# A change of order in the attention loop of a hybrid decoder layer: the last unit's scaling ahead of its neighbours, low parts and weight splits behind the probabilities

## The chip, the cores and the metric

The kernel runs on one core of a Trainium2 chip. TensorE (PE; its weight loads are listed apart as PEld), VectorE (DVE), ScalarE (ACT), GpSimd (POOL) and SyncE (SP, which here issues DMAs) each work through an instruction queue of their own and wait for one another through semaphores. The metric is the device time of one execution in microseconds; lower is better.

## The reference

One layer of a decoder for 2048 prompt tokens and 8 × 8 sample tokens. An input projection feeds a sliding-window attention (window 128, 8 query heads, 2 key heads, a learned sink per head) and a gated linear attention; both go through an output projection and are followed by a squared-ReLU MLP. The change touches the first part:

```python
h = rms_norm(x, g_mix_pre)
proj = jnp.einsum('btd,de->bte', h, w_in)
q, k, v, gq, gk, gv, gr, glr = jnp.split(proj, points, axis=-1)
q, k = rope(q...), rope(k...)
...
scores = jnp.where(mask, q @ k.T * HEAD_DIM ** -0.5, -jnp.inf)   # per head, blocks of 128
m = jnp.maximum(jnp.max(scores, axis=-1, keepdims=True), sink)
p = jnp.exp(scores - m)
p = p / (jnp.sum(p, axis=-1, keepdims=True) + jnp.exp(sink - m))
out = p @ v
```

All of it is float32. The kernel multiplies on TensorE with operands that are split into a high part and a low part (the remainder), and adds the products of the parts.

## The kernel before

The 2048 prompt tokens are 16 tiles of 128. The loop `for i in range(NB)` makes one pass per tile; what is called pass i below is the stretch from the transposes of the keys of tile i to those of tile i + 1, so it holds the last two units of tile i − 1 and the first two of tile i, and a start of the third.

**Units.** The attention of a tile is four units u0 to u3, each of two heads: `unit(i, r, jj)`, with names such as `s_7_0_0` for u0 of tile 7. A unit is a generator, and each `next` writes one step: the sink into a column of `s` (POOL); the scores `sc` (four matmuls); the row maxima `m` (two custom VectorE operations, which also write `s`); the exponentials (two on ScalarE, `s<-s,m`, each with its sum into `den`); the reciprocal of `den` and the scaling of `s` (VectorE; in u0 and u3 one of the two heads on ScalarE); the transposes `pT`; their high part `ph` (ScalarE); their low part `pl` (VectorE); the products with the values, `av` (four matmuls); half of `av` copied to `rest` (ScalarE); the sum `mo` (VectorE). Three units are under way at a time, named `behind`, `now` and `ahead` in the loop.

**Between the units.** For TensorE, `run(fill, n)` writes the next n products of the input projection of a tile further on (24 for each of its two column chunks, `proj_9_0` and `proj_9_1` for tile 9). `A_FILL` gives three numbers for each unit. A chunk's PSUM bank has tag "a", of which there are two, so the first product of a chunk needs the bank of the chunk before the last to have been read. The first unit's 11 products end with the first of a new chunk.

For the other engines, `A_PLAN` places named pieces of work at a phase (T, A, X, S, B or C, in this order) of a unit; `do(u, phase)` writes what is due:

- `first` and `rest` copy a projected tile out of PSUM, scaled by its norm `rstd_all` (ScalarE; `rest` is qk 128x248, glr and vv). `vl` writes the low parts of the values and of the gate's ranks (VectorE, vv and glr); these read the same bank.
- `turn` is the rotary step (`rotate`, GpSimd). Then `heads_T` transposes the turned queries (`pq`) and keys (`pk`) on TensorE; `lo0` and `lo1` write the queries' low parts from `pq` (VectorE, `qh<-pq,qh` and `ql<-pq,ql`), `klo0` and `klo1` the keys'.
- `x_half` transposes half of an input tile (`xT`), ScalarE takes the high part `xh`, and `x0` and `x1` are the low parts `xl` (VectorE). `xT` and `pq` have tag "d", which has a single PSUM bank.
- `junk` and `rstd` make the norm: ScalarE squares, VectorE writes `rs_v`, GpSimd writes `rstd_all`.

`split_some(n)` splits n chunks of a later projection's weights (`wg`): the early ones, 16 in all, by a GpSimd multiplication with the norm's gain, a high part on ScalarE and a low part on GpSimd; the late ones by ScalarE and VectorE.

**What sets the order.** TensorE, VectorE and ScalarE run what is written through `te`, `dv` and `ac` in the order in which it is written. GpSimd, SyncE and what is written directly to `nc.vector` (such as `load_consts`, a preparation of constants) are placed by a scheduler.

Of the kernel before, what the change touches and what calls it, by code (L numbers as in the profile page):

```python
# [25 lines left out]
NB = T // P  # L26
# [8 lines left out]
NTILE = NB + 1  # L35
# [18 lines left out]
H_EARLY, H_LATE = (1, 2), (5, 7, 6, 4, 3)  # L54
G_EARLY, G_LATE = (0, 1), (2, 3)
A_FILL = ((11, 2, 0), (10, 0, 2), (10, 0, 0), (12, 1, 0))
A_LEAD, A_SPLIT = 14, (2, 1, 0, 0)
A_PLAN = [(name, (int(at[0]), at[1])) for name, at in dict(
    klo0="3T", first="1B", hi1="3C", x1="1B", lo1="0A", klo1="0B", x0="0C", rest="3A", lo0="3A", junk="2A", turn="1A", rstd="1A", vl="3S"
).items()]  # L60
G_FIRST = (0, 1)
G_NEXT = (NB, *range(2, NB))
# [53 lines left out]
def f32(ap):  # L116
    return ap.bitcast(F32)
# [23 lines left out]
def hybrid_step_kernel(ctx: ExitStack, tc: tile.TileContext, I, O):  # L141
    nc = tc.nc
    xp = I["x_prompt"].flatten_outer_dims()
    xs = I["x_sample"].flatten_outer_dims()
    w_in = I["w_in"][0]
# [8 lines left out]
    def rows(i):  # L154
        return min(P, NTOK - i * P)

    def x_rows(i):
        return xp[i * P : (i + 1) * P, :] if i < NB else xs
# [62 lines left out]
    def split_gained(wh, wl, raw, k):  # L221
# [2 lines left out]
        ac.activation(wh, raw, AF.Copy, scale=g)  # L224
        dv.scalar_tensor_tensor(wl, raw, g, f32(wh), op0=ALU.mult, op1=ALU.subtract)

    def load_raw(stg, k, c0, n, name, tag="w_raw", bufs=2):
        raw = stg.tile([P, n], F32, tag=tag, name=f"{name}_raw{k}", bufs=bufs)
        r = slice(k * P, (k + 1) * P)
        m = min(n, G_AT - c0) if c0 < G_AT else n  # L230
        nc.sync.dma_start(raw[:, :m], w_in[r, c0 : c0 + m])
        if m < n:
            nc.sync.dma_start(raw[:, m:], w_in[r, G_AT + G_W :])
        return raw
# [13 lines left out]
    def open_gw(chunks):  # L248
        p_ = open_pool(f"g_w{chunks[0]}", "right")
        for c in chunks:  # L250
            gw[c] = (p_, *(p_.tile([P, KT, G_N], F32R, tag=f"w{c}{u}", name=f"wg{c}_{u}") for u in range(2)))
        return p_

    def load_gw(c, k, *stage):
        return c, k, load_raw(sp, k, G_AT + c * G_N, G_N, f"wg{c}", *stage)

    def split_gw(c, k, raw):
        if c in G_LATE:
            split_gained(gw[c][1][:, k, :], gw[c][2][:, k, :], raw, k)
            return  # L260
        nc.gpsimd.tensor_tensor(raw, raw, gcol[:, k : k + 1].to_broadcast([P, G_N]), op=ALU.mult)
        ac.activation(gw[c][1][:, k, :], raw, AF.Copy)
        nc.gpsimd.tensor_tensor(gw[c][2][:, k, :], raw, f32(gw[c][1][:, k, :]), op=ALU.subtract)
# [19 lines left out]
    def load_x(i):  # L283
        xs_in[i] = x = sp.tile([P, D], F32, tag="x", name=f"x_{i}", bufs=2)
        nc.sync.dma_start(x[: rows(i)], x_rows(i))
        ropes[i] = sp.tile([P, 2, HD], F32, tag="rope", name=f"rope_{i}", bufs=4)
        nc.sync.dma_start(ropes[i], I["c_rope"][i])
# [32 lines left out]
    def store():  # L320

        for dst, src in stores:
            nc.sync.dma_start(dst, src)
        stores.clear()
# [349 lines left out]
    def run(products, n=None):  # L674
        deque(products if n is None else islice(products, n), 0)
# [87 lines left out]
    def split_some(n):  # L763

        for _ in range(min(n, len(weights))):
            c, k, raw, stage = weights.popleft()
            split_gw(c, k, raw)
            if stage and late:
                weights.append((*load_gw(*late.popleft(), *stage), stage))

    early, late = (deque((c, k) for c in cs for k in range(KT)) for cs in (G_EARLY, G_LATE))
    weights = deque()
    fill = chain.from_iterable(project(i, c) for i in range(2, NTILE) for c in range(2))
# [16 lines left out]
    now, ahead, behind = next(queue), next(queue), iter(())  # L790
# [1 line left out]
        next(unit_)  # L792
    todo = {}
    for i in range(NB):
        if i + 4 < NTILE:
            load_x(i + 4)
        if i == NB - 1:
            wa_pool.release()
            w_pools.append(open_gw(G_LATE))
            for n in range(4):  # L800
                stage = ("w_raw", 2) if n % 2 else ("x", 2)
                weights.append((*load_gw(*late.popleft(), *stage), stage))
        elif i >= 3:
            for _ in range(min(2, len(early))):
                weights.append((*load_gw(*early.popleft()), None))
        store()
        if i == 4:
            nc.sync.dma_start(gain_d.rearrange("a d -> (a d)"), I["g_mix_post"][0])
            wgk, msk, smsk, dmsk, onehot, ggla = load_consts()
        if i == NB - 4:  # L810
            nc.sync.dma_start(smask, I["c_smask"])
            cached.update({(name, 0): load_cache(name, 0) for name in "kv"})
        if i >= NB - 2:
            t = i - NB + 2
            gxTs[t] = load_T(t, x_place(t))
            fill = chain(fill, projecting(t, gxTs[t], G_EARLY, ac))
        new = i + 3 < NTILE
        todo["turn"] = lambda: run(rotate(i + 1))
        if i + 2 < NTILE:
            todo["first"] = lambda: take_first(i + 2)  # L820
            todo["rest"] = lambda: todo.update(vl=take_rest(i + 2))
        if new:
            todo["junk"] = lambda: todo.update(rstd=x_norm(i + 3))

        def do(u, phase):
            for name, at in A_PLAN:
                if at == (u, phase) and name in todo:
                    todo.pop(name)()

        for u in range(4):  # L830
            next(now)
            do(u, "T")
            next(behind, None)
            next(now)
            do(u, "A")
            later = next(queue)
            next(later)
            run(fill, A_FILL[u][0])
            next(behind, None)
            if u != 3:  # L840
                next(behind, None)
            run(fill, A_FILL[u][1])
            if u == 0:
                next(now)
            if u < 2 and new:
                hi, todo[f"x{u}"] = x_half(i + 3, u)
                hi()
            elif u == 2:
                todo.update(heads_T(i + 1))
            do(u, "X")  # L850
            run(fill, A_FILL[u][2])
            if u:
                next(now)
            do(u, "S")
            if u == 3:
                next(behind, None)
            next(behind, None)
            next(ahead)
            next(now)
            do(u, "B")  # L860
            split_some(A_SPLIT[u] if i < NB - 1 else 1)
            next(now)
            do(u, "C")
            behind, now, ahead = now, ahead, later
# [3 lines left out]
    fill = chain(fill, *(projecting(t, gxTs[t], G_LATE, ac) for t in G_FIRST))  # L868
# [21 lines left out]
    for n in range(4):  # L890
# [23 lines left out]
        behind, now, ahead = now, ahead, later  # L914
# [489 lines left out]
    early = []  # L1404
    fill = chain(ending_, products())
# [451 lines left out]
    turn = [0]  # L1857
# [304 lines left out]
```

## Time and profile before

| | us |
|---|---|
| median of three runs | 2213.25 (2213.18 to 2215.95) |
| the profiled execution | 2212.31 |
| its span, from first to last instruction | 2210.4 |
| one pass of the attention loop (pass 7, 150.66 to 167.07) | 16.41 |
| passes 1 to 15, from the keys' transposes of tile 1 to those of the sample tile behind tile 15 | 48.27 to 296.60 |

The profiled execution is 0.9 us below the median of the runs. In it the granted TensorE clock is 0.995. A row of a timeline gives the start (us from the span's start), the duration, engine, line, operation, output<-inputs and the tile's shape; several alike in a row have a count, and in brackets stands the idle time ahead and what ended it. Buffer numbers are left out of the names. Nearly all rows have line 130, that of the helper that keeps the order. VectorE and ScalarE overlap the end of one instruction with the start of the next, so what one instruction costs its successor is the distance of the starts.

### The profile page before, as it was taken

What the parts mean: (1) busy time and instruction counts of PE and PEld (TensorE: products, weight loads), DVE (VectorE), ACT (ScalarE), POOL (GpSimd) and SP (SyncE); (2) the same over time, 40 slices, a digit from 0 to 9 for tenths busy, and PEclk for the clock granted to TensorE, in tenths of its full rate; (3) what the DMA queues carried; (4) which work ended last, traced back from release to release, by engine and by line L of the source; (5) the groups of instructions that cost most, each with busy time, mean ns of one, the idle gap of its engine ahead of it and who ended that gap; (6) DMA issues with size and microseconds to landing.
All of it is one profiled execution on the core that took longest, in us unless ns stands there. A gap on an engine that the chain in (4) does not pass through costs nothing.

```text
span 2210.4 us, 34115 instructions
## 1 busy us (share of the span) xinstructions
PE 2166.2 (98%) x11784; PEld 1864.2 (84%) x11784; DVE 1530.4 (69%) x3101; ACT 1220.3 (55%) x2626; POOL 262.3 (12%) x418
## 2 busy tenths in 40 slices
PE   8999999999999999899999999999999999999998
PEld 7989989999997788688888887888888888888886
DVE  5888868777785665788888655547776666555566
ACT  5889867566664443555555544435455444454454
POOL 3576512111111010000000000000000000000000
PEclk9999999999999999999999999999999999999999
DMA  7344332224336665768777677768553344666685
GB/s 228 131 143 149 102 104 65 68 80 142 126 125 219 214 217 181 240 226 274 256 271 255 248 228 225 246 187 264 175 204 139 137 154 148 229 203 197 191 271 186
DMA packets 240185, 411.53 MB, mean 186 GB/s; under 512 B 25924, under 2 KB 142124, under 8 KB 235900
## 3 DMA queue, kind: packets, MB, share of 16 engines
q1 hardware_dynamic: 240012, 409.35, 55.8%
q8 instruction: 93, 1.52, 0.3%
q14 instruction: 80, 0.66, 0.1%
HBM read 266.34 MB, written 143.99 MB: 186 GB/s over the span
## 4 chain that ended last, share of the span: by engine, by line
PE 83%; DVE 7%; ACT 5%; DMA 2%; issue 2%; POOL 1%; SPq 0%; DVEq 0%; ACTq 0%; POOLq 0%
PE dn L130 27%; PE gproj L130 9%; PE uc L130 7%; PE ua L130 7%; PE out L1306 6%; PE proj L130 5%; PE ud L130 4%; PE ub L130 4%; PE ue L130 4%; PE sam L130 1%; PE dsam L130 1%; PE av L130 1%; PE o L130 1%; PE pT L130 1%; PE sc L130 1%
## 5 line engine op out<-in xcount | busy, mean ns | idle before, releaser
L130 PE MATMUL dn<-o0t,o0s 128*128 128x512 f32 x896 | 349.1, 390 | 1.7 <-ACT f L1936 1.5
L130 PE MATMUL dn<-o1t,o0s 128*128 128x512 f32 x896 | 349.5, 390 | 0.3 <-DVE o1t L219 0.2
L130 PE MATMUL dn<-o0t,o1s 128*128 128x512 f32 x896 | 349.3, 390 | 0.0
L219 DVE TENSOR_TENSOR o1s<-rs,o0s 128x512 fp32r<-128x512 f32 x224 | 154.6, 691 | 231.0 <-ACT o0s L218 224.8
L218 ACT ACTIVATE o0s<-rs 128x512 fp32r<-128x512 f32 x224 | 141.1, 631 | 306.2 <-PE dn L130 284.0
L130 PE MATMUL gproj<-wg,gxh 128*128 128x384 f32 x1024 | 272.4, 342 | 0.3 <-DVE gp_s L213 0.3
L130 ACT ACTIVATE st<-st 128x512 f32<-128x512 f32 x224 | 141.2, 630 | 141.8 <-DVE st L130 137.8
L130 PEld LDWEIGHTS dn<-o0t,o0s 128*128 128x128 f32 x896 | 168.2, 188 | 38.6 <-ACT f L1936 1.9
L130 PEld LDWEIGHTS dn<-o1t,o0s 128*128 128x128 f32 x896 | 168.2, 188 | 37.1 <-DVE o1t L219 1.1
L130 PEld LDWEIGHTS dn<-o0t,o1s 128*128 128x128 f32 x896 | 168.2, 188 | 35.4
L130 PE MATMUL uc<-H,s 128*128 128x512 f32 x768 | 188.5, 394 | 1.7 <-ACT s L130 1.2
L130 PEld LDWEIGHTS gproj<-wg,gxh 128*128 128x128 f32 x1024 | 183.8, 188 | 4.1 <-issue 3.1
L130 PE MATMUL gproj<-wg,gxl 128*128 128x384 f32 x576 | 186.0, 340 | 0.2 <-DVE gp_s L213 0.2
L130 PE MATMUL ua<-H,w 128*128 128x512 f32 x744 | 179.2, 390 | 0.0
L130 PEld LDWEIGHTS uc<-H,s 128*128 128x128 f32 x768 | 144.2, 189 | 33.2 <-ACT s L130 1.6
L130 PEld LDWEIGHTS ua<-H,w 128*128 128x128 f32 x744 | 139.7, 188 | 29.4
L1306 PE MATMUL out<-wo,mt 128*128 128x512 f32 x680 | 160.4, 394 | 2.6 <-ACT mt L218 1.5
L219 DVE TENSOR_TENSOR o1t<-rt,o0t 128x512 fp32r<-128x512 f32 x224 | 153.3, 684 | 6.7 <-ACT o0t L218 6.7
L208 POOL TENSOR_TENSOR frs<-rs_v,half 128x1 f32<-128x1 f32 (+1 forms) x13 | 10.1, 787 | 1213.5 <-DVE rs_v L206 693.1
L1306 PEld LDWEIGHTS out<-wo,mt 128*128 128x128 f32 x680 | 127.4, 189 | 29.6 <-ACT mt L218 1.9
L218 ACT ACTIVATE o0t<-rt 128x512 fp32r<-128x512 f32 x224 | 138.3, 618 | 6.7 <-PE dn L130 3.1
L130 DVE TENSOR_TENSOR st<-st 128x512 f32<-128x512 f32 x160 | 110.6, 691 | 26.9 <-ACT st L130 22.6
(398 smaller groups left out, 4318.0 us busy)
## 6 DMA issues: line engine op xcount, KB each, us to landing
s_d<-st SPq DMA_DIRECT2D x32, 1792.0 KB, 8.5
rs<-s_d SPq DMA_DIRECT2D x224, 256.0 KB, 3.0
raw<-in_w_up SPq DMA_DIRECT2D x64, 512.0 KB, 4.4
rt<-t_d SPq DMA_DIRECT2D x128, 256.0 KB, 3.9
rt<-in_w_down SPq DMA_DIRECT2D x96, 256.0 KB, 2.8
t<-in_w_down SPq DMA_DIRECT2D x64, 256.0 KB, 3.9
t_d<-t SPq DMA_DIRECT2D x32, 512.0 KB, 3.2
hraw<-h_d SPq DMA_DIRECT2D x20, 512.0 KB, 5.4
```

The lines of the kernel that those rows point to most:

```text
L130: ins = call(*a, **k)
L208: nc.gpsimd.tensor_tensor(out, v[:n], e, op=ALU.pow)
L218: nc.scalar.activation(hi, src, AF.Copy)
L219: vector.tensor_tensor(lo, src, f32(hi), op=ALU.subtract)
L1306: te.matmul(banks[c], x, w[:, c * 512 : (c + 1) * 512], start=k + u == 0, stop=k == KT - 1 and u == len(products) - 1,)
```

## The change

Six entries and a few lines move. `rest` and `lo0` go from phase A of u3 to its phase S, behind the scaling; `vl` from phase S of u3 to phase A of the next tile's u0; `lo1` from phase A of u0 to phase S; `x0` from phase C of u0 to phase A of u1. In u3 the scores of the next unit are written behind the transposes of the unit in place of ahead of them. The weight splits move from behind phase B to behind phase A of a unit, and in all passes but the last two of them from u0 to u1. The last pass has a fill table of its own. An early pair of weight chunks is loaded ahead of the input tile.

```diff
-A_LEAD, A_SPLIT = 14, (2, 1, 0, 0)
+A_LAST = ((9, 0, 4), *A_FILL[1:])
+A_LEAD, A_SPLIT = 14, (0, 2, 1, 0)
...
-    klo0="3T", first="1B", hi1="3C", x1="1B", lo1="0A", klo1="0B", x0="0C", rest="3A", lo0="3A", junk="2A", turn="1A", rstd="1A", vl="3S"
+    klo0="3T", first="1B", hi1="3C", x1="1B", lo1="0S", klo1="0B", x0="1A", rest="3S", lo0="3S", junk="2A", turn="1A", rstd="1A", vl="0A"
...
+    fetched = []
...
-        nc.sync.dma_start(raw[:, :m], w_in[r, c0 : c0 + m])
+        fetched[:] = [nc.sync.dma_start(raw[:, :m], w_in[r, c0 : c0 + m])]
...
     for i in range(NB):
-        if i + 4 < NTILE:
+        if 3 <= i < NB - 1 and early:
+            for _ in range(min(2, len(early))):
+                weights.append((*load_gw(*early.popleft()), None))
+            with tc.issue_after(fetched[0].ins):
+                load_x(i + 4)
+        elif i + 4 < NTILE:
             load_x(i + 4)
...
-        elif i >= 3:
-            for _ in range(min(2, len(early))):
-                weights.append((*load_gw(*early.popleft()), None))
...
+        fills = A_FILL if i < NB - 1 else A_LAST
         for u in range(4):
             next(now)
             do(u, "T")
             next(behind, None)
             next(now)
             do(u, "A")
+            split_some(A_SPLIT[u] if i < NB - 1 else 1)
             later = next(queue)
             next(later)
-            run(fill, A_FILL[u][0])
+            run(fill, fills[u][0])
...
             do(u, "S")
             if u == 3:
                 next(behind, None)
             next(behind, None)
-            next(ahead)
+            if u != 3:
+                next(ahead)
             next(now)
+            if u == 3:
+                next(ahead)
             do(u, "B")
-            split_some(A_SPLIT[u] if i < NB - 1 else 1)
             next(now)
             do(u, "C")
```

In the following lists of instructions the number behind a name's unit or tile is a buffer's; `ISA` is the custom operation of the row maxima.

VectorE, from the low part of the probabilities of u3 of tile 6 to the row maxima of u1 of tile 7, before:

```order
L130 TENSOR_TENSOR pl_6_1_1_2355<-pT_6_1_1_2349,ph_6_1_1_2354 128x512
L130 SCALAR_TENSOR_TENSOR ql_7_2275<-pq_7_2267,ql_7_2275 64x512
L130 RECIPROCAL den_7_0_0_2373<-den_7_0_0_2373 128x2
L130 TENSOR_SCALAR s_7_0_0_2247<-s_7_0_0_2247,den_7_0_0_2373 128x256
L130 TENSOR_TENSOR mo_6_1984<-av_6_1_1_2391,rest_6_1_1_2396 64x256
L130 TENSOR_TENSOR kl_7_2277<-pk_7_2272,kh_7_2276 64x128
L130 TENSOR_TENSOR xl_10_2404<-xT_10_0_2405,xh_10_2403 128x512
L130 ISA s_7_0_1_2316,m_7_0_1_2434<-sc_7_0_1_2412,amask_215,sink_418 128x256
```

and after:

```order
L131 TENSOR_TENSOR pl_6_1_1_2353<-pT_6_1_1_2342,ph_6_1_1_2352 128x512
L131 SCALAR_TENSOR_TENSOR vv_8_2336<-proj_8_1_2126,rstd_all_184,vv_8_2336 128x2x64
L131 SCALAR_TENSOR_TENSOR glr_202<-proj_8_1_2126,rstd_all_184,glr_202 128x16
L131 RECIPROCAL den_7_0_0_2371<-den_7_0_0_2371 128x2
L131 TENSOR_SCALAR s_7_0_0_2247<-s_7_0_0_2247,den_7_0_0_2371 128x256
L131 SCALAR_TENSOR_TENSOR ql_7_2275<-pq_7_2267,ql_7_2275 64x512
L131 TENSOR_TENSOR mo_6_1984<-av_6_1_1_2390,rest_6_1_1_2395 64x256
L131 TENSOR_TENSOR kl_7_2277<-pk_7_2272,kh_7_2276 64x128
L131 ISA s_7_0_1_2311,m_7_0_1_2427<-sc_7_0_1_2412,amask_215,sink_418 128x256
```

The lows of tile 8's values and ranks have come in, the reading of `pq_7` by `ql_7` stands three rows further back, and the input's low part has left.

TensorE around the first transposes of an input, u0 of tile 7, has this order in both kernels (here of after):

```order
L131 MATMUL proj_9_0_2258<-wa_hi_197,xl_9_2141 128x392
L131 MATMUL proj_9_1_2388<-wa_hi_197,xh_9_2140 128x392
L131 MATMUL av_6_1_1_2390<-ph_6_1_1_2352,vv_5_1517 128x256
L131 MATMUL av_6_1_1_2390<-pl_6_1_1_2353,vv_5_1517 64x256
L131 MATMUL av_6_1_1_2390<-pl_6_1_1_2353,vv_6_1812 64x256
L131 MATMUL av_6_1_1_2390<-ph_6_1_1_2352,vv_6_1812 128x256
L131 MATMUL proj_9_1_2388<-wa_lo_198,xh_9_2140 128x392
L131 MATMUL proj_9_1_2388<-wa_hi_197,xl_9_2141 128x392
L131 MATMUL xT_10_0_2404<-ident_177,x_10_2098 128x128 x4
L131 MATMUL sc_7_0_1_2412<-kh_7_2276,qh_7_2274 128x256
```

Nothing moves here; the second row is the eleventh product of u0, which takes the bank of `proj_8_1`, and `xT_10_0` takes the bank of `pq_7`.

ScalarE, from the exponentials of u3 of tile 6 to the high part of its transposes, before:

```order
L130 ACTIVATE s_6_1_1_2189,den_6_1_1_2308<-s_6_1_1_2189,m_6_1_1_2302 128x257 x2
L130 ACTIVATE qk_8_2230<-proj_8_1_2127,rstd_all_184 128x248
L130 ACTIVATE glr_202<-proj_8_1_2127,rstd_all_184 128x2x16
L130 ACTIVATE vv_8_2313<-proj_8_1_2127,rstd_all_184 128x2x64
L130 ACTIVATE s_6_1_1_2189<-s_6_1_1_2189,den_6_1_1_2308 128x256
L130 ACTIVATE rest_6_1_0_2341<-av_6_1_0_2330 64x256
L130 ACTIVATE ph_6_1_1_2354<-pT_6_1_1_2349 128x512
```

and after:

```order
L131 ACTIVATE s_6_1_1_2189,den_6_1_1_2308<-s_6_1_1_2189,m_6_1_1_2302 128x257 x2
L131 ACTIVATE s_6_1_1_2189<-s_6_1_1_2189,den_6_1_1_2308 128x256
L131 ACTIVATE qk_8_2230<-proj_8_1_2126,rstd_all_184 128x248
L131 ACTIVATE glr_202<-proj_8_1_2126,rstd_all_184 128x2x16
L131 ACTIVATE vv_8_2336<-proj_8_1_2126,rstd_all_184 128x2x64
L131 ACTIVATE rest_6_1_0_2339<-av_6_1_0_2325 64x256
L131 ACTIVATE ph_6_1_1_2352<-pT_6_1_1_2342 128x512
```

The scaling stands ahead of the three copies, and `rest` and `ph` where they stood.

GpSimd, in a pass that splits early weights, before:

```order
L263 TENSOR_TENSOR wg1_1_193<-wg1_raw0_2362,wg1_0_192 128x384
L263 TENSOR_TENSOR wg1_1_193<-wg1_raw1_2364,wg1_0_192 128x384
L208 TENSOR_TENSOR rstd_all_184<-rs_v_2448,half_182 128x1
L261 TENSOR_TENSOR wg1_raw2_2624<-wg1_raw2_2624,gcol_185 128x384
L261 TENSOR_TENSOR wg1_raw3_2626<-wg1_raw3_2626,gcol_185 128x384
```

and after:

```order
L266 TENSOR_TENSOR wg1_1_193<-wg1_raw0_2356,wg1_0_192 128x384
L209 TENSOR_TENSOR rstd_all_184<-rs_v_2442,half_182 128x1
L266 TENSOR_TENSOR wg1_1_193<-wg1_raw1_2358,wg1_0_192 128x384
L476 COPY s_8_0_0_2509<-sink_418 128x2
L264 TENSOR_TENSOR wg1_raw2_2618<-wg1_raw2_2618,gcol_185 128x384
```

The norm has come between the two low parts.

More of the change, by code (lines that the diff above doesn't have):

```diff
@@ L841, in hybrid_step_kernel @@
                 next(behind, None)
-            run(fill, A_FILL[u][1])
+            run(fill, fills[u][1])
             if u == 0:
@@ L850, in hybrid_step_kernel @@
             do(u, "X")
-            run(fill, A_FILL[u][2])
+            run(fill, fills[u][2])
             if u:
```

## The prediction

> **What bounds the kernel now.** I read the busy time by stretches first, one stretch per pass of the attention loop, cut at the transposes of the next tile's keys (columns: span, then busy time and count of TensorE, its weight loads, VectorE, ScalarE and GpSimd, then clock, DMA share, GB/s). The stretches are passes 1, 7 and 15; the four stages behind the loop aren't touched.
>
> ```profile
> 48.27:66.44 18.17, 16.22 (x106) 14.48 (x105) 15.14 (x44) 14.10 (x41) 8.43 (x16) 1.00 0.36 115
> ...
> 150.66:167.07 16.41, 16.20 (x111) 15.32 (x110) 14.81 (x44) 14.76 (x42) 11.77 (x20) 1.00 0.40 137
> 280.75:296.60 15.85, 14.96 (x104) 14.14 (x102) 14.21 (x41) 13.43 (x38) 6.94 (x12) 1.00 0.37 115
> ```
>
> A pass takes 16.41 us at full clock. TensorE loads weights for 15.32 of it, VectorE works 14.81, ScalarE 14.76. None is full, so what counts is the order in which they hand a unit on. DMA, at a share of 0.40, isn't near its limit. So I read the timelines of the last unit of tile 6 and of the units of tile 7 (u0, u1, u2), engine by engine. TensorE first (av: probabilities times values; xT: transposes of the input of tile 10):
>
> ```profile
> 153.82 0.28 PE L130 MATMUL av<-ph,vv 128*128 128x256 f32 x1
> ...
> 154.29 0.34 PE L130 MATMUL proj<-wa_lo,xh 128*128 128x392 f32 x1
> ...
> 158.59 0.61 PE L130 MATMUL xT<-ident,x 128*128 128x128 f32 x4
> ...
> 161.76 0.28 PE L130 MATMUL av<-ph,vv 128*128 128x256 f32 x1
> 162.25 0.45 PE L130 MATMUL av<-pl,vv 128*64 128x256 f32 x2 [0.21 <-DVE rs_v L130]
> ...
> 162.65 0.60 PE L130 MATMUL xT<-ident,x 128*128 128x128 f32 x4
> ```
>
> At 153.82 four av products pass in 0.47 us; at 161.76 they take 0.89, so TensorE loses 0.42 us there. The second and third of the four read pl, the low part of the probabilities, and the row says that VectorE released them (rs_v is its next work behind pl). Now VectorE:
>
> ```profile
> 153.64 0.68 DVE L130 SCALAR_TENSOR_TENSOR qh<-pq,qh 64x512 fp32r<-64x512 f32 x1
> 154.36 0.17 DVE L130 RECIPROCAL den<-den 128x2 f32<-128x2 f32 x1
> 154.56 0.83 DVE L130 TENSOR_SCALAR s<-s,den 128x256 f32<-128x256 f32 x1
> 155.31 0.34 DVE L130 SCALAR_TENSOR_TENSOR vv<-proj,rstd_all,vv 128x128 fp32r<-128x128 f32 x1
> 155.57 0.22 DVE L130 SCALAR_TENSOR_TENSOR glr<-proj,rstd_all,glr 128x16 fp32r<-128x16 f32 x1
> 155.82 0.42 DVE L130 TENSOR_TENSOR mo<-av,rest 64x256 f32<-64x256 f32 x1
> 156.27 0.48 DVE L130 CUSTOM_DVE_ANT_0 s<-sc,amask,sink 128x256 f32<-128x256 f32 x1
> ...
> 157.80 0.69 DVE L130 SCALAR_TENSOR_TENSOR ql<-pq,ql 64x512 fp32r<-64x512 f32 x1
> 158.53 0.17 DVE L130 RECIPROCAL den<-den 128x2 f32<-128x2 f32 x1
> 158.73 0.56 DVE L130 TENSOR_SCALAR s<-s,den 128x256 f32<-128x256 f32 x1
> 159.32 0.42 DVE L130 TENSOR_TENSOR mo<-av,rest 64x256 f32<-64x256 f32 x1
> ...
> 160.10 0.69 DVE L130 TENSOR_TENSOR xl<-xT,xh 128x512 fp32r<-128x512 f32 x1
> 160.70 0.48 DVE L130 CUSTOM_DVE_ANT_0 s<-sc,amask,sink 128x256 f32<-128x256 f32 x1
> ```
>
> The reader is to see one pair: ql, the second low part of the queries, starts at 157.80 and is through at 158.49, and the xT of the TensorE rows starts at 158.59. The transposed queries pq, which ql reads, and xT share the one PSUM buffer of their tag (`bank(..., "d")`), so ql lets xT go. VectorE has ql done just in time. Last, ScalarE:
>
> ```profile
> 152.78 0.50 ACT L130 ACTIVATE s<-s,m 128x257 f32<-128x257 f32 x1
> ...
> 153.68 0.19 ACT L130 ACTIVATION_READ_ACCUMULATOR s<-s,m 128x1 f32 x1
> 153.77 0.46 ACT L130 ACTIVATE qk<-proj,rstd_all 128x248 f32<-128x248 f32 x1
> ...
> 154.56 0.51 ACT L130 ACTIVATE s<-s,den 128x256 f32<-128x256 f32 x1
> 155.09 0.38 ACT L130 ACTIVATE rest<-av 64x256 f32<-64x256 f32 x1
> ...
> 159.26 0.60 ACT L130 ACTIVATE xh<-xT 128x512 fp32r<-128x512 f32 x1
> 159.75 0.93 ACT L130 ACTIVATE wg<-wg_raw 128x384 fp32r<-128x384 f32 x2
> 160.58 0.59 ACT L130 ACTIVATE ph<-pT 128x512 fp32r<-128x512 f32 x1
> 161.28 0.51 ACT L130 ACTIVATE s<-s,m 128x257 f32<-128x257 f32 x1
> ...
> 162.19 0.19 ACT L130 ACTIVATION_READ_ACCUMULATOR s<-s,m 128x1 f32 x1
> ...
> 163.78 0.58 ACT L130 ACTIVATE qk<-proj,rstd_all 128x392 f32<-128x392 f32 x1
> ...
> 165.07 0.51 ACT L130 ACTIVATE s<-s,m 128x257 f32<-128x257 f32 x1
> ...
> 169.19 0.51 ACT L130 ACTIVATE s<-s,m 128x257 f32<-128x257 f32 x1
> ```
>
> The exponentials of the last unit start at 152.78 and, one pass on, at 169.19: 16.41, the pass. Whatever comes late between them and isn't caught up lengthens every pass.
>
> **The change, part by part.**
>
> *Scaling ahead of the copies (rest and lo0 from 3A to 3S).* After the exponentials (153.68 + 0.19 = 153.87) the reciprocal takes 0.20 (154.36 to 154.56), so the scaling can start at 154.07 in place of 154.56. ScalarE then scales (0.53, to the next start) and makes its copies, whose time is unchanged (153.77 to 154.56, 0.79): rest starts at 154.07 + 0.53 + 0.79 = 155.39, before 155.09. With 0.38 for it and 0.45 for mo (155.82 to 156.27) the row maxima of u0 come at 156.22 to 156.27: the 0.49 gained is eaten by the copies ahead of rest. The low part qh (0.72 with its gap) lies under them. Worth 0. If ScalarE could hide its copies it would be −0.49 a pass; if the scores, now behind both scaling and qh, hold TensorE, up to +0.3 (155.62, when qh would end, against the rest's 155.39). I take 0, since mo waits for rest either way.
>
> *Scores behind the transposes at u3.* The same eight instructions in the other order; the fill behind them starts when both are through. 0; up to the same 0.3 if not.
>
> *vl from 3S to 0A, lo1 from 0A to 0S.* This is the main term. Before, ql stands right behind the probabilities' low part. Now the lows of the values and ranks stand there (0.51, 155.31 to 155.82), then the reciprocal (0.20, 158.53 to 158.73), then the scaling (0.59, 158.73 to 159.32), and only then ql. It starts at 157.80 + 1.30 = 159.10, and xT, which it released 0.10 ahead of need, at 159.89 in place of 158.59. Queued behind xT on TensorE are the scores of u1, the transposes of u0's probabilities and ten projection products: all come 1.30 late. The eleventh product of u0, which needs the bank that the lows free, waits as well, but ahead of xT, so its wait is part of the same 1.30.
>
> Of this, 0.42 is recovered: av of u0 at 161.76 now comes when the low part of its probabilities is there. That leaves 1.30 − 0.42 = 0.88 at the second xT, the transposes of u1 behind it and the exponentials of u2. From 165.07 to 169.19 ScalarE has no gap to catch up in. So +0.88 a pass. The ends: +1.30 if nothing is recovered; −0.60 if xT comes in time, since x0 has left the place between mo and the maxima of u1 (160.10 to 160.70).
>
> *x0 from 0C to 1A.* Its 0.60 moves behind the low part of u0's probabilities, where VectorE would otherwise wait. At VectorE it is a loan within the pass; with xT 1.30 late it is 0, and its ends are in those just given. x1's transposes use x0's buffer: they come 0.88 late, x0's low part is through by then.
>
> *Weight splits from u0 behind B to u1 behind A.* Eight passes (16 chunks, two a pass) have them. ScalarE's two high parts leave the place ahead of ph of u0, which isn't where the time goes now: xh comes at 159.26 + 1.30 = 160.56, ph 0.60 later at 161.16, the exponentials at 161.75, through after 1.10 (161.28 to 162.38) at 162.85. Then the first high part, half of 0.93, to 163.32. On GpSimd the order is now low part, the norm's `rstd_all`, low part, where both low parts stood ahead before:
>
> ```profile
> 161.03 1.99 POOL L263 TENSOR_TENSOR wg<-wg_raw,wg 128x384 fp32r<-128x384 f32 x2
> 162.98 0.60 POOL L208 TENSOR_TENSOR rstd_all<-rs_v,half 128x1 f32<-128x1 f32 x1
> ```
>
> One low part takes 1.00, `rstd_all` 0.60: 164.92. The copy qk of the next tile, which needs it, stood at 163.78: 1.14 late, and ph of u1 and the exponentials of u2 stand behind it on ScalarE. So these eight passes lose 1.14 in place of 0.88. Low end: 0.88, if the norm overtakes; high end: 1.9, if the second low part delays it too (0.88 + 1.00).
>
> *Pass 1.* VectorE's preparation of constants falls beside GpSimd's rotary step there, and is slower than its like ahead of it:
>
> ```profile
> 45.02 0.41 DVE L649 TENSOR_TENSOR c_raw<-c_raw,wgk 32x256 f32<-32x256 f32 x1 [0.23 <-ACT wgk L647]
> ...
> 52.28 1.15 DVE L649 TENSOR_TENSOR c_raw<-c_raw,wgk 32x256 f32<-32x256 f32 x1
> ```
>
> After the change two such operations come ahead of that step. The pass is 18.17 − 16.41 = 1.76 above pass 7; if that goes but for two operations of 0.41, and 0.88 comes, it is −0.06: 0, from −0.9 (1.76 gone) to +0.9 (nothing gone). The Trainium skill, SBUF — State Buffer, section "Who interferes with whom", says that a VectorE operation with two SBUF inputs and a GpSimd one that reads SBUF exclude each other; the pair 0.41 and 1.15 agrees, and by that rule the low end is the nearer one.
>
> *Pass 14* has no inputs left to transpose, so no xT to hold; only the eleventh product waits: the lows' 0.51 less nothing gained, +0.4 (0 to 0.5). *Pass 15* splits one chunk in every unit, and the low part is VectorE's there:
>
> ```profile
> 289.91 0.69 DVE L130 SCALAR_TENSOR_TENSOR wg<-wg_raw,gcol,wg 128x384 fp32r<-128x384 f32 x1
> ```
>
> It moves from behind the transposes to ahead of the reciprocal: 4 × 0.69 = 2.8 at most, and less VectorE's idle time of that pass, 15.85 − 14.21 = 1.64, at least 1.1. Between: +2.0. The new fill (9, 0, 4) of its first unit shifts two products and adds none: 0, covered by the other four; ±0.4 at the price of a pair.
>
> *Loads.* Each x tile is issued behind two weight loads. It is read one pass later; that cover, 16 us, hides it, and without it its transposes wait. 0.
>
> *Sum.* Passes 2 to 13 are twelve: 8 × 1.14 = 9.1 and 4 × 0.88 = 3.5; pass 1: 0; pass 14: 0.4; pass 15: 2.0. Together +15.0 on the profiled execution's 2212.3: 2227.3. The median of the runs is 0.9 above that execution, so 2228.2.
>
> **The rivals.** *Faster:* xT isn't late. It decides whether ql ends by 158.49, for which the maxima of u0 would have to come 1.30 earlier than at 156.27. Then x0's 0.60 leaves the way and 12 × −0.60 = −7.2, with 2.4 for passes 14 and 15: 2208.4. For it speaks that the low part of the queries can wait; against it the sums of the scaling part, which find nothing earlier. 0.14.
>
> *No change:* TensorE is the bound at 15.32 of 16.41, its instructions are the same, its queue has products to fill in. Then passes 14 and 15 and pass 1's gain remain, 2.4 − 0.9 = +1.5: 2214.7. Against it: TensorE keeps its order, and nothing stands between the wait and the transposes that could be taken first. The Trainium skill, Perfetto Trace Analysis, section "Identifying the Most-Contended Engine", would have TensorE judged by its weight loads, here 93% of the pass, and so speaks for this case; the 0.42 lost at one av says that the hand-over decides too. 0.12.
>
> *Slower by less:* ScalarE and TensorE catch up half of 0.88 and the norm overtakes on GpSimd: 12 × 0.44 + 2.4 = 7.7, 2220.9. For it: the idle 1.09 of TensorE per pass (16.41 − 15.32), of which I gave back only 0.42. 0.20.
>
> **How the numbers follow.** The forecast as summed has 0.54: 2228.2, by itself from 2225 (twelve passes at 0.88, pass 15 at its low end) to 2235 (eight passes at 1.88, pass 15 at its high end). 0.2% is 4.4 us, about what a measurement of this kernel can tell from no change; so slower takes the forecast and the smaller loss, 0.74, same the second rival, 0.12, faster the first, 0.14. The range leaves the faster case and a tail above: 2213 to 2235.
>
> **What would show it.** The first xT of a pass stands right behind ql at about 1.1 us of TensorE's idle time, released by VectorE; the eleventh product waits for the rank's low part; the wait in av of u0 is gone; qk in split passes is released by GpSimd; passes at 17.3 to 17.55. I am wrong if the first xT starts as early after the exponentials as now, 5.81 us (152.78 to 158.59), or if a pass stays at 16.41.

## The result and the profile after

The changed kernel takes 2230.5 us (median), the kernel before 2213.4; the ratio is 1.0077, with a 95% interval of 1.0066 to 1.0089. That is 17.1 us or 0.77% slower, against a forecast of 2228.2. The profiled execution took 2229.58 (span 2227.8), 17.3 more than that of before. One of the changed kernel's six runs took 7071 us and is left out of the ratio; the median of the other five is 2230.3. Passes 1, 7 and 15 of the changed kernel, in the view of busy time by stretches:

```profile
49.02:67.42 18.40, 16.12 (x105) 14.57 (x104) 14.04 (x44) 14.10 (x41) 8.21 (x16) 1.00 0.33 110
156.59:173.95 17.36, 16.64 (x112) 15.32 (x111) 14.58 (x44) 14.94 (x41) 11.69 (x20) 1.00 0.39 132
293.93:311.67 17.74, 15.47 (x103) 14.14 (x102) 13.61 (x39) 13.62 (x38) 6.88 (x12) 1.00 0.33 104
```

The engines have nearly the same to do: pass 7 grows from 16.41 to 17.36 with the same 15.32 us of weight loads, 0.18 more on ScalarE and 0.23 less on VectorE. TensorE's timeline in pass 7 shows where it now waits (the exponentials of u3 start at 158.86; the kernel before has the same point at 152.78):

```profile
164.42 0.42 PE L131 MATMUL proj<-wa_hi,xh 128*128 128x392 f32 x1 [0.53 <-DVE glr L131]
...
165.61 0.66 PE L131 MATMUL xT<-ident,x 128*128 128x128 f32 x4
...
168.82 0.28 PE L131 MATMUL av<-ph,vv 128*128 128x256 f32 x1
168.94 0.39 PE L131 MATMUL av<-pl,vv 128*64 128x256 f32 x2
...
169.29 0.41 PE L131 MATMUL xT<-ident,x 128*128 128x128 f32 x2
```

The eleventh product waits for the low part of the ranks. The first xT comes 6.75 us after the exponentials, before 5.81. The four av products pass in 0.47 us, as forecast, where they took 0.89. The second xT is 10.43 after the exponentials, before 9.87: 0.56 late. VectorE's timeline in the same pass:

```profile
162.37 0.48 DVE L131 CUSTOM_DVE_ANT_0 s<-sc,amask,sink 128x256 f32<-128x256 f32 x1
...
163.79 0.34 DVE L131 SCALAR_TENSOR_TENSOR vv<-proj,rstd_all,vv 128x128 fp32r<-128x128 f32 x1
164.05 0.22 DVE L131 SCALAR_TENSOR_TENSOR glr<-proj,rstd_all,glr 128x16 fp32r<-128x16 f32 x1
164.29 0.17 DVE L131 RECIPROCAL den<-den 128x2 f32<-128x2 f32 x1
164.49 0.35 DVE L131 TENSOR_SCALAR s<-s,den 128x256 f32<-128x256 f32 x1
164.86 0.69 DVE L131 SCALAR_TENSOR_TENSOR ql<-pq,ql 64x512 fp32r<-64x512 f32 x1
...
169.31 1.41 DVE L131 TENSOR_SCALAR s<-s,den 128x256 f32<-128x256 f32 x2
```

ScalarE's, from the exponentials of u3 to those of u2:

```profile
158.86 0.50 ACT L131 ACTIVATE s<-s,m 128x257 f32<-128x257 f32 x1
...
170.89 0.59 ACT L131 ACTIVATE qk<-proj,rstd_all 128x392 f32<-128x392 f32 x1 [0.23 <-POOL rstd_all L209]
...
172.08 0.51 ACT L131 ACTIVATE s<-s,m 128x257 f32<-128x257 f32 x1
```

And GpSimd's, with the rotary step's large last operation, the low part of a weight chunk and the norm:

```profile
164.59 1.40 POOL L403 TENSOR_TENSOR rot<-qk,tb 128x512 f32<-128x512 f32 x1
...
169.29 1.01 POOL L266 TENSOR_TENSOR wg<-wg_raw,wg 128x384 fp32r<-128x384 f32 x1 [1.78 <-ACT wg L131]
170.25 0.60 POOL L209 TENSOR_TENSOR rstd_all<-rs_v,half 128x1 f32<-128x1 f32 x1
```

The order of VectorE is the one that the prediction reckoned with: ql stands four rows further back than before, behind the two lows, the reciprocal and the scaling, and starts 6.00 after the exponentials in place of 5.02. The exponentials of u2 come at 13.22 (172.08 − 158.86) in place of 12.29: 0.93 late, which is what the pass has grown by.

### The profile page after: what moved, and what is told of

It reads as the page before. It is cut to its first block, busy times and chain, and to the rows that moved or that the text cites. A ratio compares the mean times of both kernels' runs of the same rounds, so it can differ in the third digit from the quotient of the medians.

```text
span 2227.8 us, 34113 instructions
## 1 busy us (share of the span) xinstructions
PE 2172.3 (98%) x11784; PEld 1864.2 (84%) x11784; DVE 1524.7 (68%) x3101; ACT 1221.2 (55%) x2626; POOL 260.8 (12%) x418
## 4 chain that ended last, share of the span: by engine, by line
PE 78%; ACT 8%; DVE 8%; DMA 3%; issue 2%; POOL 1%; SPq 0%; DVEq 0%; ACTq 0%; POOLq 0%
PE dn L131 26%; PE gproj L131 8%; PE uc L131 7%; PE ua L131 7%; PE out L1315 6%; PE ud L131 4%; PE ub L131 4%; PE ue L131 4%; PE proj L131 2%; ACT s L131 2%; PE sam L131 1%; PE dsam L131 1%; DVE s L131 1%; PE o L131 1%; DMA hraw<-h_d 1%
```

## The experiments

Each of the twelve kernels has its ratio to the kernel before from runs of the same set. There are three sets (four kernels that undo parts, four with one part alone, and the last four), in which the kernel before has 2213.7, 2214.0 and 2213.5. The last two columns are passes of the profiled executions, one for each kernel: pass 7, which splits weights, and pass 12, which doesn't.

| kernel | median us | ratio to before, 95% | pass 7 | pass 12 |
|---|---|---|---|---|
| before | 2213.4 | | 16.41 | 16.41 |
| changed | 2230.5 | 1.0077 (1.0066 to 1.0089) | 17.36 | 16.98 |
| lo1 and vl back | 2226.1 | 1.0062 (1.0048 to 1.0076) | 17.11 | 16.79 |
| vl back | 2232.9 | 1.0087 (1.0074 to 1.0099) | 17.34 | 16.96 |
| lo1 back | 2227.7 | 1.0065 (1.0053 to 1.0077) | 17.19 | 16.80 |
| splits back | 2228.1 | 1.0065 (1.0053 to 1.0077) | 17.38 | 16.96 |
| before + scaling part | 2222.8 | 1.0045 (1.0031 to 1.0058) | 17.10 | 17.10 |
| before + x0 | 2213.3 | 0.9997 (0.9988 to 1.0005) | 16.44 | 16.08 |
| before + lows | 2229.0 | 1.0070 (1.0058 to 1.0082) | 17.70 | 17.71 |
| before + splits | 2222.7 | 1.0038 (1.0023 to 1.0053) | 16.75 | 16.39 |
| scaling part, rotary held | 2217.2 | 1.0019 (1.0010 to 1.0029) | 16.80 | 16.39 |
| lows, xT in another bank | 2225.4 | 1.0052 (1.0039 to 1.0066) | 17.14 | 17.14 |
| before + x0 + loads | 2212.6 | 0.9994 (0.9985 to 1.0003) | 16.42 | 16.11 |
| the same, rotary held | 2214.3 | 1.0004 (0.9995 to 1.0013) | 16.75 | 15.99 |

**Undoing parts of the change.** First both pieces of which the prediction made its main term:

```diff
-    lo1="0S" ... vl="0A"
+    lo1="0A" ... vl="3S"
```

> The changed kernel with two of its entries undone: lo1 at 0A (ql directly behind pl) and vl at 3S (lows ahead of the row maxima of u0). In the changed kernel's pass 7 the eleventh product comes 5.56 us after the exponentials of u3 (before 4.72) and xT 6.75 us after them (before 5.81). Theory T (late lows and a late ql together hold TensorE): xT is back at 5.8 to 5.9, passes 5 to 10 fall from 17.34 to 16.3 to 16.5, and the time is some 11 us below the changed kernel, 2217 to 2221. Rival W (the weight splits and the norm on GpSimd make the loss): passes without splits fall, passes 5 to 10 stay at 17.0 or more, 2226 to 2229.

xT is back at 6.04, yet passes 6 to 10 fall only to 17.1 (pass 5 stays at 17.44), and the time by 4.5 us in place of 11, with intervals that overlap. Theory T misses here, and rival W has the size nearly right, but not its reason, as the fourth run shows. Something else costs nearly as much once the lows are out of the way. VectorE's timeline of this kernel in pass 7 has the scaling of u0, which takes 0.35 in the changed kernel:

```profile
163.57 1.03 DVE L131 TENSOR_SCALAR s<-s,den 128x256 f32<-128x256 f32 x1
```

What slows it is the question of the run with the scaling part alone. Before that, each piece alone:

```diff
-    vl="0A"
+    vl="3S"
```

> The changed kernel with vl alone back at 3S; lo1 stays behind the scaling. Theory T (two holds side by side, each good for nearly the whole delay): the eleventh product is back at 4.7 to 4.9 us after the exponentials of u3, but ql still ends where it does, since the reciprocal ahead of it waits for the exponentials of u0, and xT stays at 6.6 to 6.8; the time stays within 2 us of the changed kernel. Rival P (the eleventh product alone): xT at 6.0 to 6.1, 8 us faster than the changed kernel. By the prediction's own sum (ql late by 0.51 + 0.20 + 0.59), 0.51 less a pass: 6 us faster.

The time is 2.4 us above the changed kernel's, a little outside T's 2 us, with intervals that overlap, and not 6 or 8 below it. TensorE's wait has only moved, from the eleventh product to xT, which stays at 6.74. TensorE's timeline of this kernel in pass 7:

```profile
167.26 0.66 PE L131 MATMUL xT<-ident,x 128*128 128x128 f32 x4 [0.54 <-DVE ql L131]
```

```diff
-    lo1="0S" ... vl="0A"
+    vl="0A", lo1="0A"
```

> The changed kernel with lo1 alone back at 0A, written behind vl: VectorE does pl, the two lows, ql, then the reciprocal and the scaling. Theory T: ql ends 6.1 us after the exponentials of u3 in place of 6.7, but the eleventh product still comes at 5.56 and xT, five instructions of work behind it, at 6.6; the time stays within 2 us of the changed kernel. Rival Q (the bank of pq alone): xT at 6.2, 0.55 less a pass, 7 us faster than the changed kernel.

ql ends at 6.13, and xT still comes at 6.63, behind the product that the lows hold, in TensorE's timeline of this kernel:

```profile
163.72 0.41 PE L131 MATMUL proj<-wa_hi,xh 128*128 128x392 f32 x1 [0.53 <-DVE glr L131]
...
164.79 0.60 PE L131 MATMUL xT<-ident,x 128*128 128x128 f32 x4
```

So in the changed kernel two holds stand side by side, each good for nearly the whole lateness of xT; the prediction put the eleventh product inside the other one, and either alone would do. The 2.8 us gained here are a little more than was expected, with intervals that overlap: xT and what follows come 0.1 to 0.2 earlier in most passes, pass 1 falls to 16.91 and pass 15 to 17.06, and pass 4 grows to 21.43.

```diff
-A_LEAD, A_SPLIT = 14, (0, 2, 1, 0)
+A_LEAD, A_SPLIT = 14, (2, 1, 0, 0)
...
             do(u, "A")
-            split_some(A_SPLIT[u] if i < NB - 1 else 1)
...
             do(u, "B")
+            split_some(A_SPLIT[u] if i < NB - 1 else 1)
```

> The changed kernel with the weight splits alone undone: behind phase B again, two in u0 and one in u1, and behind B in the last pass too. Theory T: xT stays at 6.75; passes 5 to 10 lose what the norm on GpSimd costs, 17.34 to 17.0 to 17.15 (six to eight passes, 2 us), pass 15 falls from 17.74 to about 16 and pass 4 from 20.30 to about 19.5: 4 to 6 us faster than the changed kernel, 2225 to 2227. Rival W: passes 5 to 10 fall to 16.5, 12 us faster.

Passes 5 to 10 stay at 17.38: both theories expected some gain there, and there is none; the time is 2.4 us lower, with intervals that overlap, where T had 4 to 6. With the splits ahead of ph again, the exponentials of u1 come at 9.24 in place of 8.86, and what the norm and the low parts gave back is lost there. Pass 15 falls from 17.74 to 16.09 and pass 4 from 20.30 to 19.29, which is all that the splits cost the changed kernel.

**One part alone.** The scaling part had been reckoned at nothing:

```diff
-    rest="3A", lo0="3A"
+    rest="3S", lo0="3S"
...
-            next(ahead)
+            if u != 3:
+                next(ahead)
             next(now)
+            if u == 3:
+                next(ahead)
             do(u, "B")
```

> The kernel before with one part of the change: rest and lo0 at 3S behind the scaling, and the scores of u3 behind its transposes; vl, lo1, x0, the splits and the loads as before. Theory T (the prediction's sums: copies ahead of rest eat the gain, nothing else changes): the row maxima of u0 come 3.5 to 3.7 us after the exponentials of u3, a pass costs at most 0.2 more, 0 to +3 us. Theory L (VectorE's scaling stands still while GpSimd works on two SBUF operands; the copy qk comes 0.74 later, so the rotary step does, and its last third falls on the scaling of u0): that scaling takes about 1.0 in place of 0.56, the maxima of u1 come 0.5 to 0.7 later, +6 to +8 us.

+0.63 to +0.71 in passes 2, 3 and 6 to 15, and +8.8 us: T falls for this part, and L gives the size. (Pass 1 is 1.3 shorter, pass 4 2.3 longer, pass 5 0.4 longer.) The copy qk of the last unit starts 1.73 after the exponentials in place of 0.99. The rotary step on GpSimd, which reads it, comes later by as much, and its large last operation lies on the scaling of u0. VectorE's timeline of this kernel in pass 7:

```profile
161.94 1.03 DVE L130 TENSOR_SCALAR s<-s,den 128x256 f32<-128x256 f32 x1
```

GpSimd's at the same time:

```profile
161.53 1.28 POOL L400 TENSOR_TENSOR rot<-qk,tb 128x512 f32<-128x512 f32 x1
```

The scaling begins 0.41 after the rotary operation, and ends 0.16 after it, at 162.97. The row maxima of u1 come at 8.61 in place of 7.92.

```diff
-    x0="0C"
+    x0="1A"
```

> The kernel before with x0 alone at 1A. Theory T: the row maxima of u1 come 0.5 to 0.6 earlier, but the exponentials of u1 stand behind ph of u0 on ScalarE and stay; the 0.42 lost at av of u0 goes; 0 to -0.2 a pass, -2.5 to 0 us. Rival (x0 is in the way in its new place: it stands ahead of the reciprocal of u1): +0.3 to +0.6 a pass, +4 to +7 us.

No difference in the time (0.9997), as T has it: the maxima of u1 come 0.60 earlier, and in passes with splits nothing is made of it. In pass 12 it is −0.33. Pass 1 is 1.7 shorter and pass 4 1.9 longer, and the two cancel; what the 1.7 are is told with the run that adds the loads.

```diff
-    lo1="0A" ... vl="3S"
+    lo1="0S" ... vl="0A"
```

> The kernel before with vl at 0A and lo1 at 0S alone. Theory T: the eleventh product comes 5.5 us after the exponentials of u3 (before 4.72) and xT at 6.7 to 7.1 (before 5.81); 0.8 to 1.2 a pass and 11 to 15 us. Rival (the late lows are absorbed, as the removal of both in the changed kernel gave back only 4 us): a pass at most 0.4 longer, up to +5 us.

T holds: 15.0 us or 0.70% slower, 1.3 a pass. TensorE's timeline of this kernel in pass 7 says by what it is held (the exponentials of u3 start at 160.64):

```profile
165.77 0.45 PE L130 MATMUL proj<-wa_hi,xh 128*128 128x392 f32 x1 [0.24 <-DVE glr L130]
...
167.92 0.66 PE L130 MATMUL xT<-ident,x 128*128 128x128 f32 x4 [0.88 <-DVE ql L130]
```

Here the scaling of u0 lies beside the rotary operation as well (0.80), so ql starts at 6.53 and xT at 7.28.

```diff
-A_LEAD, A_SPLIT = 14, (2, 1, 0, 0)
+A_LEAD, A_SPLIT = 14, (0, 2, 1, 0)
...
             do(u, "A")
+            split_some(A_SPLIT[u] if i < NB - 1 else 1)
...
             do(u, "B")
-            split_some(A_SPLIT[u] if i < NB - 1 else 1)
```

> The kernel before with the weight splits alone at their new places (behind phase A, two in u1 and one in u2, and behind phase A in the last pass; its fill as before). Theory T (the norm behind a late low part on GpSimd): 0.25 in each of eight passes, 1 in pass 4, 2 in pass 15: +4 to +5 us. Theory L: the low parts fall on the scaling of u1, which takes 1.0 in place of 0.56, 0.5 in each of eight passes: +7 to +8 us. If the splits cost only beside a late xT (their removal from the changed kernel left passes 5 to 10 as they were): passes 5 to 10 at 16.4 to 16.5, +2 to +3 us.

+0.33 to +0.44 in passes 5 to 8 and 10 and +0.69 in pass 9, +2.6 in pass 4, +0.5 in pass 15; all passes add up to some 6 us. The median is 9 above that of before, the ratio 0.38% (0.23 to 0.53). The size lies between T's and L's, the median nearer L's; the place is L's. The two scalings of u1 in VectorE's timeline of the kernel before:

```profile
162.61 0.82 DVE L130 TENSOR_SCALAR s<-s,den 128x256 f32<-128x256 f32 x2
```

And of this kernel:

```profile
166.38 1.42 DVE L130 TENSOR_SCALAR s<-s,den 128x256 f32<-128x256 f32 x2
```

They stand beside the first of the two low parts of the weights in GpSimd's:

```profile
166.10 0.67 POOL L208 TENSOR_TENSOR rstd_all<-rs_v,half 128x1 f32<-128x1 f32 x1 [1.26 <-DVE rs_v L130]
166.64 2.02 POOL L263 TENSOR_TENSOR wg<-wg_raw,wg 128x384 fp32r<-128x384 f32 x2
```

The norm doesn't stand behind a low part here, so the price isn't the one that the prediction named.

**The two causes by themselves.** To hold the rotary operation behind the scaling, with all else as in the scaling part alone:

```diff
+        if r == jj == 0:
+            firsts[i] = s
...
         rots[i] = rot = sp.tile([P, 5, 2, HD], F32, tag="rot", name=f"rot_{i}", bufs=1)
+        if i - 1 in firsts:
+            nc.gpsimd.tensor_copy(rot[:1, 0, 0, :1], firsts.pop(i - 1)[:1, 1, :1])
```

> The scaling part alone (as the run before last, pass 17.10), with a GpSimd copy of one element of u0's scaled tile into the rotary step's output, so that the large last operation of that step (1.28 us) starts behind the scaling of u0 and not beside it; nothing on VectorE, ScalarE or TensorE differs. Theory L (VectorE's scaling stands still while GpSimd's operation runs): the scaling of u0 takes 0.4 to 0.6 in place of 1.03, the row maxima of u1 come 8.0 to 8.2 us after the exponentials of u3 in place of 8.61, passes 16.55 to 16.75, 4 to 6 us faster than without the copy: 2217 to 2219. Rival (the scaling is slow or late for another reason; the scaling part costs by its own order): passes stay at 17.0 to 17.1, 2222.

Passes 2 and 12 are back at 16.41 and 16.39, all that the scaling part had cost there; passes 13 and 14 keep 0.20 and 0.41 of it. The time falls by 5.6. VectorE's timeline of this kernel in pass 7:

```profile
159.35 0.36 DVE L130 TENSOR_SCALAR s<-s,den 128x256 f32<-128x256 f32 x1
```

And GpSimd's:

```profile
159.84 0.18 POOL L401 COPY rot<-s 1x1 f32<-1x1 f32 x1 [0.43 <-DVE s L130]
160.09 1.30 POOL L402 TENSOR_TENSOR rot<-qk,tb 128x512 f32<-128x512 f32 x1
```

The same instruction on the same tile takes 0.36 alone and 1.03 beside the rotary operation. Passes with splits stay at 16.80: GpSimd now starts the low parts of the weights 9.10 after the exponentials, in the kernel before 8.25, and the scaling of u1, back at 9.84 as before, falls on them.

To take the hold of ql off xT, with all else as in the lows' part alone:

```diff
-                hi, todo[f"x{u}"] = x_half(i + 3, u)
+                hi, todo[f"x{u}"] = x_half(i + 3, u, "d" if u else "c")
```

> The lows' part alone (vl at 0A, lo1 at 0S; pass 17.69), with xT of the first half of an input in the banks of the probabilities' transposes (two of them) in place of the single bank it shares with pq; no order differs. Theory T (xT is held by ql through that bank): xT comes at 5.9 to 6.2 us after the exponentials of u3 in place of 7.28, the row maxima of u1 at 8.4 to 8.7 in place of 9.21, passes 17.0 to 17.2, 6 to 8 us faster: 2221 to 2223. Rival (VectorE's own order sets the pass, the bank is only near it): xT early, but passes stay at 17.5 or more.

xT comes at 6.23, before ql has started, which it does at 6.55 as with the lows alone, and the passes fall from 17.70 to 17.14. TensorE's timeline of this kernel in pass 7, and VectorE's:

```profile
165.27 0.60 PE L130 MATMUL xT<-ident,x 128*128 128x128 f32 x4
```

```profile
165.59 0.69 DVE L130 SCALAR_TENSOR_TENSOR ql<-pq,ql 64x512 fp32r<-64x512 f32 x1
...
167.70 0.48 DVE L130 CUSTOM_DVE_ANT_0 s<-sc,amask,sink 128x256 f32<-128x256 f32 x1
```

So the bank holds xT, and this hold costs 0.56 a pass there. The other 0.73 of the lows' 1.29 stays, and the rival has that much right: VectorE still does the two lows and a slowed scaling ahead of ql and mo, and the row maxima of u1 come at 8.66 (167.70 − 159.04), 0.74 later than before. The time falls by 3.6 us, less than the 6 to 8 expected: 12 × 0.56 is 6.7, but pass 4 is 1.4 longer in this kernel (20.86 against 19.50).

**A version without the costly parts.**

```diff
-    x0="0C"
+    x0="1A"
...
+        if 3 <= i < NB - 1 and early:
+            for _ in range(min(2, len(early))):
+                weights.append((*load_gw(*early.popleft()), None))
+            with tc.issue_after(fetched[0].ins):
+                load_x(i + 4)
+        elif i + 4 < NTILE:
             load_x(i + 4)
```

> The kernel before with two parts of the change that cost nothing by themselves: x0 at 1A and the weights' loads ahead of the input tile's. By the run of x0 alone: passes 1, 2 and 11 to 13 keep its gain (1.7 and 0.2 to 0.3 each), passes 5 to 10 stay at 16.4. If the order of the loads matters for pass 4 (20.51 with x0 alone, 18.62 before, 19.29 with the changed kernel's loads and the splits back), that falls to 18.5 and the time to 2210 or 2211; if not, 2212 to 2213.

Pass 4 is 20.03, and the time, 0.9994 (0.9985 to 1.0003), not distinguishable from before. The order of the loads isn't what makes pass 4.

The gain in pass 1, which the expectation counted on, isn't kept: the pass takes 18.48, with x0 alone 16.46, although the instructions of VectorE, ScalarE, GpSimd and TensorE have the same order up to there. VectorE's preparation of constants and the first operation of GpSimd's rotary step start within 0.01 us of each other in both. With x0 alone, on VectorE and on GpSimd:

```profile
52.80 0.42 DVE L649 TENSOR_TENSOR c_raw<-c_raw,wgk 32x256 f32<-32x256 f32 x1
```

```profile
52.79 1.15 POOL L391 TENSOR_TENSOR tb<-qk,rope 128x320 f32<-128x320 f32 x1 [0.83 <-POOL kl L450]
```

And with the loads:

```profile
53.06 1.15 DVE L651 TENSOR_TENSOR c_raw<-c_raw,wgk 32x256 f32<-32x256 f32 x1
```

```profile
53.05 0.87 POOL L393 TENSOR_TENSOR tb<-qk,rope 128x320 f32<-128x320 f32 x1 [0.83 <-POOL kl L452]
```

One of the two waits for the other, and which one does goes with 2 us of pass 1. So the 1.7 us of x0 alone are not x0's. How often the tie falls either way is not shown, since one execution of each kernel is profiled.

To this the hold of the rotary operation is added:

```diff
+            firsts[i] = s
...
+        if i - 1 in firsts:
+            nc.gpsimd.tensor_copy(rot[:1, 0, 0, :1], firsts.pop(i - 1)[:1, 1, :1])
```

> The last kernel with the large rotary operation held behind the scaling of u0 as in the first of this set. Theory L: the scaling of u0 takes 0.36 in place of 0.56 and the row maxima of u1 come up to 0.2 earlier; the exponentials of u1 stand behind ph of u0 on ScalarE in the eight passes with splits, so 0 to 0.1 there, 0.1 to 0.2 in the others: 0 to 2 us faster than the last kernel.

The scaling of u0 is faster (0.36 in place of 0.57), the maxima of u1 come 0.21 earlier, and pass 12 is 15.99; but the eight passes with splits grow to 16.75, as with the hold before, and the sum is 1.0004. None of these beats the kernel before clearly.

## Why the prediction was right

The time, the sign and the size came out: 2228.2 forecast, 2230.5 measured. In the profiled executions passes 1 to 15 grew by 14.3 us, where 15.0 were forecast. The other 3.0 us of the difference lie ahead of pass 1 (0.75) and behind pass 15; executions of the kernel before differ by 6.3 us among themselves (2210.3 to 2216.6 in the last set), so no cause is sought for them.

- **Scaling ahead of the copies: the row maxima of u0 are not moved.** Right: 3.51 after the exponentials, before 3.49. That the part is worth 0 was wrong. The step that failed is the one that costed the copies by ScalarE alone. It took no account of who reads qk: the rotary step on GpSimd, and through it the scaling of u0. Alone, the part costs 0.69 a pass. In the whole change it doesn't show at this place in passes 7 and 12, since the scaling of u0 then starts ahead of the rotary operation (in pass 7 at 164.49, 0.10 ahead) and takes 0.35; in passes 1 and 14 it does.
- **xT 1.30 late, by 0.51 + 0.20 + 0.59.** With the lows alone the mechanism is shown by the wait of 0.88 on ql and by the run with another bank. In the changed kernel the sign that the prediction named for it, some 1.1 us of idle time ahead of xT, is missing: the idle time, 0.53, stands ahead of the eleventh product, and ql's hold shows only when that product is let go (0.54 with vl back). The size is 0.94 (6.75 against 5.81): the 0.59 was a scaling that had been slowed beside GpSimd, and it took 0.37 from start to start here. That the eleventh product's wait is only a part of the same lateness was incomplete: it is a second hold of nearly equal length, which remains when ql's is taken away.
- **0.42 recovered at av of u0.** Right, 0.47 for the four products.
- **0.88 in passes without splits.** Too much: 0.57 to 0.82 in passes 2 and 11 to 13. The 0.94 less the 0.42 is 0.52, and 0.56 is what the second xT shows.
- **1.14 in passes with splits, by the norm on GpSimd.** Passes 5 to 10 grew by 0.94, pass 3 by 0.79. The copy qk did come 1.03 late (12.03 against 11.00), released by `rstd_all`. But undoing the splits in the changed kernel gave nothing back in these passes, and the splits alone cost 0.35 where the norm came early. What this part adds is the low parts' collision with the scaling of u1 (1.41 in place of 0.82), and the old place has a price of like size beside a late xT. The step's reason fell; its size came near because one price took the place of another.
- **Pass 1, 0:** +0.23. The gain that was reckoned came: VectorE's two preparations of constants take 0.42 each, where they took 1.15 and 1.41. It is lost again at a place that no term had: the scaling of u0 takes 1.48 there, beside the rotary step's large operation.
- **Pass 14, +0.4:** +1.38, mis-sized. The scaling part costs 0.67 there and the lows 0.70, each by itself; the scaling of u0 takes 1.29 in place of 0.56.
- **Pass 15, +2.0:** +1.89. Putting the splits back takes 1.65 of it away, as the step has it; by themselves on the kernel before they cost 0.53 there, so most of the 1.65 is made together with other parts. The fill table of the last pass is in both kernels of the first comparison and in neither of the second; by itself it was not tried.
- **Pass 4** was counted among those with splits and grew by 1.68. It lies between 18.6 and 21.6 in all these kernels. In the kernel before ScalarE waits 2.03 us there for GpSimd's multiplication of a weight chunk; what moves it from kernel to kernel stays open.

The sum was partly luck. Passes 3 to 10 cost 8.1 us, where 9.1 were reckoned, and passes 2 and 11 to 13 cost 2.7 in place of 3.5, since the lateness of xT was put too high; pass 14 cost 1.0 more than reckoned, of which the scaling part, put at nothing, makes 0.67 by itself, and the 3.0 us outside the passes were in no term.

The parts don't add: alone they cost 0.69, 0.03, 1.29 and 0.34 in pass 7, 2.35 together, and the whole change costs 0.95. The timelines of pass 12, which has no splits, show two reasons. The scaling of u0, slowed to 0.81 with the lows alone and to 1.03 with the scaling part alone, takes 0.35 in the changed kernel, because the two together put it just ahead of the rotary operation. And x0 has left the place ahead of the maxima of u1, which come at 7.91 as in the kernel before, with the lows alone at 9.21. What is left is the late xT: the second one is 0.56 late in pass 7, and pass 12 costs 0.57. How the saving divides between the two reasons is not shown; no run has the lows with only one of them. Nor does any run take both holds off the changed kernel and keep its scaling undisturbed.

Of the rivals, the faster case needed ql to end in time, which it didn't. TensorE as the bound fails by its own row, 15.32 us of weight loads in a pass of 17.36. The smaller loss, half of 0.88, is below what the passes show.

## What to carry to other kernels

When work is moved on one engine, list not only what waits for the moved instruction's result but what waits for its operands: a low part that is the last reader of a PSUM bank lets go the next user of the bank, and moving it behind a scaling held TensorE for 0.88 us in the kernel with the lows alone. When two engines can block each other, a part costed at nothing can move an operation onto another engine's: look at what runs beside an instruction that takes 0.36 us at one place and 0.56 or 1.03 at another before its duration goes into a sum. And where two waits end close together, undoing one of them shows nothing; here only undoing both brought xT back. A gain in a pass whose length hangs on a tie between two engines is not yet the change's: the 1.7 us of pass 1 with x0 alone were gone in a kernel with the same order.

## What the runs showed of the hardware

VectorE's scaling of a float32 tile of 128 x 256, SBUF to SBUF with one factor for each partition, takes 0.34 to 0.36 us when GpSimd is idle or starts clearly later. When it starts during a GpSimd operation of 128 x 320 to 128 x 512 with two SBUF operands it ends 0.15 to 0.16 after that operation: at 162.97 behind 162.81 with the scaling part alone, at 159.29 behind 159.14 in the kernel before. Where it starts first, by 0.10 us, it keeps its 0.35 and the GpSimd operation takes 1.40 in place of 1.28. The Trainium skill, SBUF — State Buffer, section "Who interferes with whom", says that a VectorE operation of this kind in its two-port mode and a GpSimd operation exclude each other for a whole instruction, whichever comes first; both directions agree with it here. That the scaling runs in this mode is not shown. Which of the two comes first can't always be told from the starts in the profile: in pass 1 of the changed kernel the scaling starts at 57.05, 0.05 ahead of the rotary operation, and takes 1.48, and the tie of pass 1 above fell both ways. That the exclusion decides the whole price of one part in some passes (0.69 in pass 12, gone when the rotary operation was held) was not expected.
